# State space input products from stacked 96-row operands, and the skip term on VectorE

## The chip, the cores and the metric

One core of one Trainium2 chip. The metric is the device time of one execution in microseconds, the median of the runs; a profiled execution of the same program gives the trace. TensorE multiplies, VectorE and ScalarE work elementwise, GpSimd here issues a few DMAs and clears buffers, and SyncE issues most DMAs.

## What is computed

Two layers of a hybrid block on 272 rows (16 learned tokens and 256 of the input) of width 1024. A layer is: half a SwiGLU FFN (width 2816), a token mixer, another half FFN. The mixer runs one input projection, and two branches from it: forgetting attention with 8 heads, and a state space branch (S5). Cut to what the change touches, the state space branch is:

```python
# u: (L, 512), 32 groups of 16 channels, 64 complex states in each
bu_re = einsum('lgc,gpc->lgp', ug, b_re)      # the input products
bu_im = einsum('lgc,gpc->lgp', ug, b_im)
...                                           # scaled, then a scan over l
y = einsum('lgp,gcp->lgc', h_re, c_re) - einsum('lgp,gcp->lgc', h_im, c_im) \
    + d_skip.reshape(32, 16) * ug             # the skip term
y = gelu(y.reshape(L, 512))
z = y @ w_glu
out = z[..., :512] * sigmoid(z[..., 512:])
```

## The kernel before

Activations are held transposed: 128 channels on the partitions, the 272 rows along the free dimension. Every float32 product is made of three products of rounded parts (a high part and the rest, `hi` and `lo`): high by high, high by low, low by high. Lines 296 to 298 (`unit`) issue these for all large weights: one unit is 8 blocks of 128, so 24 matmuls. The weights stream from HBM through SyncE in file order; `Weights.high` (L156, ScalarE) rounds a unit and `Weights.low` (L169, VectorE) subtracts to get its low half, three to four units ahead of its use.

The order of instructions is written by the program itself. `tick()` is called after a unit: it prepares the weights of a later unit, runs the functions that `later(n, ...)` put off to this tick, and then lets the background go on. The background is a generator that yields a cost after each of its steps; a tick gives it a budget (900 in the FFN, 1600 in the Q, K, V stage, 2700 and 2600 beside the gates), and a yield of -1 ends its turn for this tick. `mids` are functions that run in the middle of the next unit of 8 blocks (at i == MID == 6), which is where the matmuls of the background stand. `finish_background()` runs whatever is left of it at once.

In the first FFN of layer 0 the background makes constants of the state space model (`ssm_setup`) and then the tables of layer 0 (`ssm_tables(0)`): the matrix B in two parts (`Bh`, `Bl`), powers for the rotations (`E`, by doubling, L599 to L609, with a squaring of 11 small operations between doublings), the output matrix (`Cx`, L617 to L631), and a diagonal matrix of the skip weights in two parts (`Dh`, `Dl`, L635 and L637). The FFN has 68 ticks (two for each of 22 column blocks, three for each of 8 output blocks), and the background starts at the eighth. The second FFN of layer 0 makes the tables of layer 1 in the same way, without the setup.

In the mixer the background is `ssm_branch`. A layer has 16 steps j in four blocks m. Step j: `bu` makes the input products, three matmuls for the real and three for the imaginary part, on the 32 partitions of `uh(m)`, `ul(m)` that belong to j; VectorE rotates them (`turn`, L676 into `p`), adds and subtracts (L728, L730), scans (L740) and rotates back (L676 into `m`). The next step's `bu` is asked for when the rotation into `p` is done, since there is one PSUM buffer for it. After four steps `out_m` makes an output block: three matmuls with the diagonal matrix for the skip term (L658 to L660) and 24 with `Cx` (L666), which ScalarE stores (L698). After the Q, K, V units (f, V0 to V3, eight of K and Q) and 16 gate units come two `branch_b` units, then `finish_background`, GELU and the GLU product.

`uh`, `ul` and `yr` (output) are slots of 128x4x272 from a pool of 18, given out in order of return.

Of the kernel before, what the change touches and what calls it, by code (L numbers as in the profile page):

```python
# [7 lines left out]
F32 = mybir.dt.float32  # L8
# [31 lines left out]
WARM = 10  # L40
START = 8
BLOCK = 1024
MASKED = -float(2.0 ** 100)
O_U, O_Q, O_K, O_V, O_F, O_G = 0, 512, 1024, 1536, 2048, 2056
MAGIC = 12582912.0
# [133 lines left out]
def body(tc, nc, ins, out):  # L179
    v, s, pe = nc.vector, nc.scalar, nc.tensor  # L180

    with (
# [7 lines left out]
    ):  # L190
        names = iter(range(10**6))

        halves = Slots(mp, "m", 18, [P, 4, T])
        banks = Slots(pp, "ps", 6, [P, 512])
        temps = Slots(tp, "t", 6, [P, T])
        bank, tmp = banks.take, temps.take
# [1 line left out]
        def big(n, dt=F32):  # L198
            return Tiles(halves, n, dt)
# [330 lines left out]
            yield SMALL  # L530

        E = cp.tile([P, 2, NJ, TS + 1], F32, name="E")
        Bh = cp.tile([P, 2, 4, P], F32R, name="Bh")
        Bl = cp.tile([P, 2, 4, P], F32R, name="Bl")
        Cx = cp.tile([P, 4, NJ, 32], F32, name="Cx")
        Dh = cp.tile([P, 4, P], F32R, name="Dh")
        Dl = cp.tile([P, 4, P], F32R, name="Dl")

        def ssm_tables(l):

            js = slice(l * NJ, (l + 1) * NJ)
            bslot = halves.take()
            Bm = bslot.rearrange("p a t -> p (a t)")[:, : 8 * P].rearrange("p (r m c) -> p r m c", r=2, m=4)
            nc.sync.dma_start(Bm, ins["B"][l])
            yield -1
            yield -1
            for r in range(2):
                s.copy(Bh[:, r], Bm[:, r])
                yield -1
                v.tensor_sub(Bl[:, r], Bm[:, r], Bh[:, r].bitcast(F32))  # L550
                yield 600
            halves.give(bslot)
            cslot = halves.take()
            Cm = cslot.rearrange("p a t -> p (a t)")[:, : 2 * NJ * 32].rearrange("p (r j c) -> p r j c", r=2, j=NJ)
            nc.sync.dma_start(Cm, ins["C"][l])
# [75 lines left out]
            v.tensor_scalar(Cx[:, 3], Cx[:, 2], -1.0, None, ALU.mult)  # L631
            yield 600
            halves.give(cslot)
            for m in range(4):
                s.activation(Dh[:, m], ident, AF.Copy, scale=pc("d", l, m))  # L635
                yield -1
                v.scalar_tensor_tensor(Dl[:, m], ident, pc("d", l, m), Dh[:, m].bitcast(F32), ALU.mult, ALU.subtract)  # L637
                yield 200


        def ssm_branch(l, uh, ul, yr, t0, ready):
            n = T - t0

            def bu(j):
                pb = bp.tile([P, 2, 512], F32, tag="b2", name=f"bu{next(names)}")
                m, q = divmod(j, 4)
                rows = slice(32 * q, 32 * q + 32)
                for r in range(2):
                    a, b, x, y = Bh[rows, r, m, :], Bl[rows, r, m, :], uh(m)[rows], ul(m)[rows]
                    pe.matmul(pb[:, r, :T], lhsT=a, rhs=x, start=True, stop=False)  # L650
                    pe.matmul(pb[:, r, :T], lhsT=a, rhs=y, start=False, stop=False)  # L651
                    pe.matmul(pb[:, r, :T], lhsT=b, rhs=x, start=False, stop=True)  # L652
                return pb

            def out_m(m, qt):
                ps = bank()
                a, b, x, y = Dh[:, m], Dl[:, m], uh(m)[:, t0:], ul(m)[:, t0:]
                pe.matmul(ps[:, :n], lhsT=a, rhs=x, start=True, stop=False)  # L658
                pe.matmul(ps[:, :n], lhsT=a, rhs=y, start=False, stop=False)
                pe.matmul(ps[:, :n], lhsT=b, rhs=x, start=False, stop=False)  # L660
                for x, row, a, b, stop in (
                    (0, 3, t0, TS, False), (3, 2, t0, TS, False), (1, 3, TS, T, False), (2, 2, TS, T, False),
                    (0, 0, t0, T, False), (2, 1, t0, T, True),
                ):
                    for q in range(4):
                        pe.matmul(  # L666
                            ps[32 * q : 32 * q + 32, a - t0 : b - t0], lhsT=Cx[:, x, 4 * m + q, :],
                            rhs=qt[q][:, row, a:b], start=False, stop=stop,
                        )
# [12 lines left out]
            pbs = {}  # L682

            def ask(j):
                mids.append(lambda: pbs.__setitem__(j, bu(j)))

            def shut(m, qt):


                def finish():  # L690
                    if not banks.free:
                        mids.append(finish)
                        return
                    ps = out_m(m, qt)
                    halves.give(*qt)

                    def store():
                        s.copy(yr(m)[:, t0:], ps[:, :n])  # L698
                        stored.append(m)
                        banks.give(ps)  # L700

                    later(1, store)

                mids.append(finish)

            while 0 not in ready:
                yield -1
            ask(0)
            g, qt = None, []
            for j in range(NJ + 1):  # L710
                back = iter(())
                if j < NJ:
                    p = buf("p", 1, [P, 4, T])
                    while j not in pbs:
                        yield -1
                    yield from turn(p, pbs.pop(j)[:, :, :T], j)
                    if j + 1 < NJ:
                        assert (j + 1) // 4 in ready
                        ask(j + 1)
                if j:  # L720
                    while not halves.free:
                        yield -1
                    qt.append(halves.take())
                    back = turn(qt[-1], g, j - 1)
                    yield next(back)
                if j < NJ:
                    c, d = (x.rearrange("p r (s t) -> p (r s) t", s=2) for x in (p[:, :2], p[:, 2:]))
                    v.tensor_add(c[:, 1:3], c[:, 1:3], d[:, 3::-3])  # L728
                    yield 352
                    v.tensor_sub(c[:, 0::3], c[:, 0::3], d[:, 2:0:-1])  # L730
# [18 lines left out]
        def mixer(l, hh, hl, t0, finish):  # L749
# [10 lines left out]
                    v.scalar_tensor_tensor(dst[:, lo:], ps[:, : T - lo], by, rstd[:, lo:], ALU.mult, ALU.mult)  # L760
                banks.give(ps)

            ready = set()

            def have_u(ps, m):
                u = tmp()
                scaled(ps, u, 0)

                def done():
                    temps.give(u)  # L770
                    ready.add(m)

                split(uh(m), ul(m), u, done)

            state["bg"] = ssm_branch(l, uh, ul, yr, t0, ready)
            state["budget"] = QKV_BUDGET
            for m in range(4):
                if m == 0:
# [267 lines left out]
                stored.clear()  # L1046

            bias(0)
            yb = big(8, F32R)
            gB, gA = big(8), None  # L1050
            for i in range(16):
                state["budget"] = GATE_BUDGET if i < 11 else LATE_BUDGET
# [15 lines left out]

                later(1, e)
                if 5 <= i < 12 and i % 2 == 1:  # L1070
                    values((i - 5) // 2)
                if 3 <= i < 11:
                    flip(i - 3)
# [38 lines left out]
            flush()  # L1112
            gelus()
            flush()
            for x in (uh, ul, yr):
                x.give()

            zg = big(8, F32R)
            for m in range(4):
# [287 lines left out]


def _ssm_mats(inp):
    B = np.zeros((DEPTH, P, 2, 4, P), np.float32)  # L1410
    C = np.zeros((DEPTH, P, 2, NJ, 32), np.float32)
    for r, (kb, kc) in enumerate((("ssm_b_re", "ssm_c_re"), ("ssm_b_im", "ssm_c_im"))):
        for gi in range(2):
            b = inp[kb].reshape(DEPTH, 4, 4, 2, 64, 16)[:, :, :, gi]
            for q in range(4):
                rows = slice(q * 32 + gi * 16, q * 32 + gi * 16 + 16)
                B[:, rows, r, :, gi * 64 : gi * 64 + 64] = b[:, :, q].transpose(0, 3, 1, 2)
            c = inp[kc].reshape(DEPTH, NJ, 2, 16, 64)[:, :, gi]
            C[:, gi * 64 : gi * 64 + 64, r, :, gi * 16 : gi * 16 + 16] = c.transpose(0, 3, 1, 2)
    return B, C  # L1420


# [26 lines left out]
```

## Time and profile before

| | |
|---|---|
| median of 3 runs | 1227.82 us (1227.7 to 1228.13) |
| profiled execution | 1226.46 us |
| its span, first to last instruction | 1224.7 us |
| mean granted clock of TensorE | 0.998 of full speed |
| TensorE busy | 1212.0 us, 99% |
| VectorE busy | 928.7 us, 76% |
| ScalarE busy | 637.1 us, 52% |

The difference between the profiled execution and its span, 1.76 us, lies around the first and last instruction. Busy times of TensorE are of pipelined matmuls whose ends are modelled: successive starts are 0.12 us apart where one takes 0.29 us in the rows, so starts are what to compare.

### The profile page before, as it was taken

Reading aid. Unit: us, or ns where it says so; the run is one execution under the profiler, and the core shown is the slowest. Engines: PE = TensorE matmul, PEld = TensorE weight load, DVE = VectorE, ACT = ScalarE, POOL = GpSimd, SP = SyncE. Lnnn points to the kernel's source line nnn. Section 1 sums busy time; section 2 is a strip of 40 time slices with the busy share of each in tenths; the row PEclk is TensorE's granted clock in tenths of the full one; section 3 lists DMA queues with packets and bytes.
Section 4 is the critical chain, followed back from the end, with each engine's and each line's share of the span. In section 5 each row is a group of like instructions: output and inputs, shape, how many; then the busy total and the mean of one; then the engine's idle time right before and its main releaser. Section 6 shows DMA issues by size and latency. Waiting matters only on the chain.

```text
span 1224.7 us, 24247 instructions
## 1 busy us (share of the span) xinstructions
PE 1212.0 (99%) x9905; PEld 1183.3 (97%) x9905; DVE 928.7 (76%) x1718; ACT 637.1 (52%) x1056; POOL 6.0 (0%) x12
## 2 busy tenths in 40 slices
PE   9999999999999999999999999999999999999997
PEld 8999999999889999999999999999998999999997
DVE  6978898998888798886565555559989897666553
ACT  7544444636557564444454444446475676544542
POOL 0000000000000000000000000000000000000000
PEclk9999999999999999999999999999999999999999
DMA  7756554543334665555556555554422355655551
GB/s 236 214 195 192 160 175 153 164 135 98 88 104 155 205 193 188 173 168 172 177 172 177 176 176 166 172 160 154 140 100 97 111 173 172 224 189 183 173 183 65
DMA packets 56479, 199.27 MB, mean 163 GB/s; under 512 B 6288, under 2 KB 6672, under 8 KB 56368
## 3 DMA queue, kind: packets, MB, share of 16 engines
q1 hardware_dynamic: 55872, 196.96, 51.5%
q8 instruction: 77, 1.26, 0.4%
q10 hardware_dynamic: 416, 0.62, 0.1%
q14 instruction: 34, 0.28, 0.1%
q0 software_dynamic: 80, 0.15, 0.0%
HBM read 196.66 MB, written 1.05 MB: 161 GB/s over the span
## 4 chain that ended last, share of the span: by engine, by line
PE 94%; DVE 3%; ACT 1%; issue 1%; DMA 1%; SPq 0%; DVEq 0%; ACTq 0%
PE ps L296 29%; PE ps L298 29%; PE ps L297 28%; PE ps L666 1%; DVE wl L169 1%; PE bu L650 1%; PE ps L965 1%; PE bu L651 1%; PE bu L652 1%; DMA raw<-wts 1%; PE ps L968 0%; ACT wh L156 0%; ACT m L1089 0%; PE ps L1030 0%; DVE p L676 0%
## 5 line engine op out<-in xcount | busy, mean ns | idle before, releaser
L296 PE MATMUL ps<-m,wh 128*128 128x272 f32 (+2 forms) x2960 | 856.5, 289 | 0.8 <-ACT wh L156 0.6
L298 PE MATMUL ps<-m,wl 128*128 128x272 f32 (+2 forms) x2960 | 849.5, 287 | 0.4 <-DVE wl L169 0.4
L297 PE MATMUL ps<-m,wh 128*128 128x272 f32 (+2 forms) x2960 | 847.0, 286 | 0.6 <-DVE m L315 0.3
L156 ACT CAST wh<-raw 128x1024 fp32r<-128x1024 f32 (+2 forms) x380 | 388.6, 1025 | 451.3 <-issue 235.6
L296 PEld LDWEIGHTS ps<-m,wh 128*128 128x128 f32 (+1 forms) x2960 | 556.3, 188 | 10.8 <-issue 5.6
L297 PEld LDWEIGHTS ps<-m,wh 128*128 128x128 f32 (+1 forms) x2960 | 556.2, 188 | 1.9 <-DVE m L315 0.8
L298 PEld LDWEIGHTS ps<-m,wl 128*128 128x128 f32 (+1 forms) x2960 | 556.4, 188 | 1.1 <-DVE wl L169 0.9
L169 DVE TENSOR_TENSOR wl<-raw,wh 128x1024 fp32r<-128x1024 f32 (+2 forms) x380 | 450.2, 1186 | 54.6 <-PE ps L298 43.9
L389 DVE TENSOR_TENSOR t<-t,ps 128x272 f32<-128x272 f32 (+1 forms) x88 | 38.1, 433 | 77.0 <-PE ps L298 75.2
L383 DVE TENSOR_TENSOR t<-ps,rstd 128x272 f32<-128x272 f32 (+1 forms) x88 | 38.3, 436 | 43.5 <-PE ps L298 42.9
L676 DVE TENSOR_TENSOR p<-bu,E 128x544 f32<-128x544 f32 x64 | 44.4, 719 | 8.6 <-PE bu L652 6.3
L676 DVE TENSOR_TENSOR m<-g,E 128x544 f32<-128x544 f32 x64 | 45.7, 717 | 2.7 <-PE ps L666 2.7
L740 DVE TENSOR_TENSOR_SCAN g<-ssm_mag,p 128x272 f32<-128x272 f32 x64 | 42.8, 710 | 0.7
L391 ACT CAST m<-t 128x272 fp32r<-128x272 f32 (+1 forms) x88 | 36.1, 410 | 12.6 <-DVE t L389 12.5
L417 DVE TENSOR_TENSOR t<-ps,rstd 128x272 f32<-128x272 f32 (+1 forms) x32 | 14.0, 437 | 36.9 <-PE ps L298 36.6
L394 DVE TENSOR_TENSOR m<-t,m 128x272 fp32r<-128x272 f32 (+1 forms) x88 | 37.9, 431 | 3.6 <-ACT m L391 3.6
L384 ACT ACTIVATE t<-t 128x272 f32<-128x272 f32 (+1 forms) x88 | 37.1, 422 | 6.1 <-DVE t L383 6.0
L329 ACT ACTIVATE m<-h,par 128x272 fp32r<-128x272 f32 (+1 forms) x48 | 24.5, 518 | 12.5 <-DVE h L419 7.2
L332 DVE SCALAR_TENSOR_TENSOR m<-h,par,m 128x272 fp32r<-128x272 f32 (+1 forms) x48 | 23.4, 494 | 8.5 <-ACT m L329 8.3
L354 DVE RECIPROCAL rstd<-t 128x272 f32<-128x272 f32 (+1 forms) x6 | 11.0, 1836 | 21.4 <-ACT t L353 21.4
L312 ACT CAST m<-t 128x272 fp32r<-128x272 f32 (+1 forms) x32 | 13.1, 415 | 19.9 <-DVE t L1167 15.4
L650 PE MATMUL bu<-m,Bh 32*128 32x272 f32 x64 | 21.4, 335 | 2.0 <-DVE p L676 2.0
(228 smaller groups left out, 709.1 us busy)
## 6 DMA issues: line engine op xcount, KB each, us to landing
raw<-wts SPq DMA_DIRECT2D x344, 512.0 KB, 3.6
raw<-wts SPq DMA_DIRECT2D x32, 384.0 KB, 3.4
h<-hT SPq DMA_DIRECT2D x4, 272.0 KB, 5.0
m<-B SPq DMA_DIRECT2D x2, 512.0 KB, 4.8
m<-C SPq DMA_DIRECT2D x2, 512.0 KB, 5.0
out<-m SPq DMA_DIRECT2D x2, 256.0 KB, 2.1
out<-m ACTq DMA_DIRECT2D x1, 512.0 KB, 2.8
raw<-wts SPq DMA_DIRECT2D x2, 128.0 KB, 2.0
```

The source lines that it names most:

```text
L156: nc.scalar.copy(hi[:, c : c + w // parts], r[:, c : c + w // parts])
L169: nc.vector.tensor_sub(lo[:, k], r[:, k], hi[:, k].bitcast(F32))
L296: pe.matmul(ps[:width, :n], lhsT=a, rhs=mh, start=first and i == ks[0], stop=False)
L297: pe.matmul(ps[:width, :n], lhsT=a, rhs=ml, start=False, stop=False)
L298: pe.matmul(ps[:width, :n], lhsT=b, rhs=mh, start=False, stop=last and i == ks[-1])
L383: v.tensor_mul(x[:, :n], pg[:, :n], rstd[:, t0:])
L384: s.activation(y[:, :n], x[:, :n], AF.Silu)
L389: v.tensor_mul(y[:, :n], y[:, :n], pu[:, :n])
L391: s.copy(ah(f)[:, t0:], y[:, :n])
L394: v.tensor_sub(al(f)[:, t0:], y[:, :n], ah(f)[:, t0:].bitcast(F32))
L676: v.tensor_tensor(d[:, :, :, a : a + TS], x[:, :, a : a + TS].unsqueeze(1).to_broadcast([P, 2, 2, TS]), tab.unsqueeze(2).to_broadcast([P, ...
L740: v.tensor_tensor_scan(g[:, r], mg, p[:, r], 0.0, ALU.mult, ALU.add)
```

## The change

B is laid out on the host in 32 rows, and three copies of these rows are stacked to 96. On the chip, `ssm_tables` loads it in four parts; rows 0 to 63 are rounded (two high copies), and rows 64 to 95 become the low part. The input of a step is stacked in the same way: high, low, high. One matmul over 96 rows then sums what three matmuls over 32 rows did, so a step has two matmuls in place of six. The stacked inputs are made by DMAs from SBUF to SBUF on GpSimd's queue, twelve for each block m, into a slot of their own; block 0 is declared ready two ticks after its DMAs are issued (`DELAY`). The diagonal matmuls go, and the skip term is added in the store, on VectorE, from `u` kept in `yr`. The pool has 19 slots, and `yb` is taken later.

```diff
+BROWS = 96
+DELAY = 2
-        halves = Slots(mp, "m", 18, [P, 4, T])
+        halves = Slots(mp, "m", 19, [P, 4, T])
-        Bh = cp.tile([P, 2, 4, P], F32R, name="Bh")
-        Bl = cp.tile([P, 2, 4, P], F32R, name="Bl")
+        Bs = cp.tile([BROWS, NJ, 2 * P], F32R, name="Bs")
-        Dh = cp.tile([P, 4, P], F32R, name="Dh")
-        Dl = cp.tile([P, 4, P], F32R, name="Dl")
         def ssm_tables(l):
-            bslot = halves.take()
-            Bm = bslot.rearrange("p a t -> p (a t)")[:, : 8 * P].rearrange("p (r m c) -> p r m c", r=2, m=4)
-            nc.sync.dma_start(Bm, ins["B"][l])
-            yield -1
-            yield -1
-            for r in range(2):
-                s.copy(Bh[:, r], Bm[:, r])
-                yield -1
-                v.tensor_sub(Bl[:, r], Bm[:, r], Bh[:, r].bitcast(F32))
-                yield 600
-            halves.give(bslot)
+            top = BROWS - 32
+            for j in range(0, NJ, 4):
+                x = Bs[:, j : j + 4].rearrange("p j c -> p (j c)")
+                slots = halves.take(), halves.take(F32R)
+                raw, hi = (y.rearrange("p a t -> p (a t)")[:BROWS, : 8 * P] for y in slots)
+                nc.sync.dma_start(raw, ins["B"][l][:, j * 2 * P : (j + 4) * 2 * P])
+                yield -1
+                yield -1
+                s.copy(x[:top], raw[:top])
+                s.copy(hi[top:], raw[top:])
+                yield -1
+                v.tensor_sub(x[top:], raw[top:], hi[top:].bitcast(F32))
+                yield 1200
+                halves.give(*slots)
...
-            for m in range(4):
-                s.activation(Dh[:, m], ident, AF.Copy, scale=pc("d", l, m))
-                yield -1
-                v.scalar_tensor_tensor(Dl[:, m], ident, pc("d", l, m), Dh[:, m].bitcast(F32), ALU.mult, ALU.subtract)
-                yield 200
...
             def bu(j):
                 for r in range(2):
-                    a, b, x, y = Bh[rows, r, m, :], Bl[rows, r, m, :], uh(m)[rows], ul(m)[rows]
-                    pe.matmul(pb[:, r, :T], lhsT=a, rhs=x, start=True, stop=False)
-                    pe.matmul(pb[:, r, :T], lhsT=a, rhs=y, start=False, stop=False)
-                    pe.matmul(pb[:, r, :T], lhsT=b, rhs=x, start=False, stop=True)
+                    pe.matmul(pb[:, r, :T], lhsT=Bs[:, j, r * P : r * P + P], rhs=us[m](q)[:BROWS], start=True, stop=True)
+                if q == 3:
+                    us[m].give()
...
             def out_m(m, qt):
-                a, b, x, y = Dh[:, m], Dl[:, m], uh(m)[:, t0:], ul(m)[:, t0:]
-                pe.matmul(ps[:, :n], lhsT=a, rhs=x, start=True, stop=False)
-                pe.matmul(ps[:, :n], lhsT=a, rhs=y, start=False, stop=False)
-                pe.matmul(ps[:, :n], lhsT=b, rhs=x, start=False, stop=False)
...
                     def store():
-                        s.copy(yr(m)[:, t0:], ps[:, :n])
+                        y = yr(m)[:, t0:]
+                        v.scalar_tensor_tensor(y, y, pc("d", l, m), ps[:, :n], ALU.mult, ALU.add)
...
             def have_u(ps, m):
-                u = tmp()
-                scaled(ps, u, 0)
+                scaled(ps, yr(m), 0)
                 def done():
-                    temps.give(u)
-                    ready.add(m)
+                    x = big(4, F32R)
+                    for q in range(4):
+                        for i, part in enumerate((uh, ul, uh)):
+                            nc.gpsimd.dma_start(
+                                x(q)[32 * i : 32 * i + 32].bitcast(F32), part(m)[32 * q : 32 * q + 32].bitcast(F32)
+                            )
+                    later(DELAY if m == 0 else 0, lambda: us.__setitem__(m, x))
+                    if m == 3:
+                        uh.give()
+                        ul.give()
-                split(uh(m), ul(m), u, done)
+                split(uh(m), ul(m), yr(m), done)
...
-            yb = big(8, F32R)
+            yb = None
...
                 if 5 <= i < 12 and i % 2 == 1:
+                    yb = yb or big(8, F32R)
```

## Rows read from the trace of the kernel before

**Rows 1.** Part 1 of the page: busy time, share of the span, instructions.

```profile
PE 1212.0 (99%) x9905; PEld 1183.3 (97%) x9905; DVE 928.7 (76%) x1718; ACT 637.1 (52%) x1056; POOL 6.0 (0%) x12
```

**Rows 2.** Stretches, first to last rotation in each layer's mixer: length, busy times, clock.

```profile
224.10:361.40 137.30, 136.46 (x1152) 124.46 (x1153) 122.46 (x212) 72.99 (x163) 0.00 (x0) 1.00 0.38 114
...
837.20:969.60 132.40, 131.20 (x1123) 120.01 (x1123) 121.33 (x206) 72.84 (x160) 0.00 (x0) 1.00 0.35 117
```

**Rows 3.** VectorE's waits in these two stretches: us in total, times, longest.

```profile
DVE mx L975 <- PE ps L968: 4.5, 3, 2.1
...
DVE m L760 <- PE ps L298: 0.3, 1, 0.3
...
DVE mx L975 <- PE ps L968: 3.9, 3, 2.0
...
DVE m L886 <- PE ps L298: 0.6, 1, 0.6
```

**Rows 4.** Timeline of TensorE, one step's input products: start, us, what.

```profile
222.85 0.28 PE L298 MATMUL ps<-m,wl 128*32 128x272 f32 x1
223.07 0.39 PE L650 MATMUL bu<-m,Bh 32*128 32x272 f32 x1
...
224.01 0.31 PE L296 MATMUL ps<-m,wh 128*32 128x272 f32 x1
```

**Rows 5.** Timeline of TensorE, an output block.

```profile
268.55 0.29 PE L658 MATMUL ps<-m,Dh 128*128 128x272 f32 x1
...
269.02 2.05 PE L666 MATMUL ps<-m,Cx 128*32 128x136 f32 x48
```

**Rows 6.** VectorE by line and shape, 163 to 212 us: count, busy, mean ns, idle.

```profile
L169 DVE TENSOR_TENSOR wl<-raw,wh 128x1024 fp32r<-128x1024 f32 x12 | 14.6, 1219 | 0.6 <-issue 0.6
...
L417 DVE TENSOR_TENSOR t<-ps,rstd 128x272 f32<-128x272 f32 x6 | 2.6, 439 | 0.9 <-PE ps L298 0.7
...
L603 DVE TENSOR_TENSOR E<-vn 128x256 f32<-128x256 f32 x4 | 1.7, 424 | 0.1
...
L617 DVE TENSOR_TENSOR Cx<-m,ssm_kr 128x512 f32<-128x512 f32 x1 | 0.7, 684 | 0.0
...
L599 DVE TENSOR_TENSOR vn<-E,s_a 128x144 f32<-128x144 f32 x1 | 0.3, 300 | 0.0
...
L579 DVE TENSOR_TENSOR s_r<-s_r,s_dt 128x16 f32<-128x16 f32 x1 | 0.2, 168 | 0.0
```

**Rows 7.** Timeline of VectorE at the end of layer 0's first FFN.

```profile
211.12 1.13 DVE L637 SCALAR_TENSOR_TENSOR Dl<-rcon,par,Dh 128x128 fp32r<-128x128 f32 x4
```

**Rows 8.** Timeline of TensorE: unit u3's first low product, first of unit f.

```profile
217.96 0.29 PE L298 MATMUL ps<-m,wl 128*128 128x272 f32 x1
...
220.73 0.29 PE L296 MATMUL ps<-m,wh 128*32 128x272 f32 x1
```

**Rows 9.** GpSimd's DMA issue on the timeline; DMA issues, KB, us to landing.

```profile
2.45 0.54 POOL L1220 DMA_DIRECT2D m<-conr  x1
...
m<-conr POOLq DMA_DIRECT2D x1, 136.0 KB, 5.0
```

**Rows 10.** Timeline of VectorE around the last rotation of layer 0.

```profile
360.05 1.36 DVE L676 TENSOR_TENSOR m<-g,E 128x544 f32<-128x544 f32 x2
361.33 0.79 DVE L1088 TENSOR_TENSOR m<-m,rstd 128x272 f32<-128x272 f32 x2
362.03 1.14 DVE L315 TENSOR_TENSOR m<-m,m 128x272 fp32r<-128x272 f32 x3
363.09 1.22 DVE L169 TENSOR_TENSOR wl<-raw,wh 128x1024 fp32r<-128x1024 f32 x1
364.22 0.79 DVE L1088 TENSOR_TENSOR m<-m,rstd 128x272 f32<-128x272 f32 x2
```

**Rows 11.** Timeline of TensorE, start of the last output block, both layers.

```profile
363.90 0.29 PE L658 MATMUL ps<-m,Dh 128*128 128x272 f32 x1
...
971.19 0.28 PE L658 MATMUL ps<-m,Dh 128*128 128x256 f32 x1
```

**Rows 12.** Stretches at the end of the kernel: busy times, clock behind them.

```profile
1219.50:1220.00 0.50, 0.00 (x0) 0.00 (x0) 0.50 (x1) 0.43 (x1) 0.00 (x0) 1.00 0.00 0
1220.00:1220.50 0.50, 0.00 (x0) 0.00 (x0) 0.13 (x1) 0.50 (x2) 0.00 (x0) 0.50 0.27 102
```

More of the change, by code (lines that the diff above doesn't have):

```diff
@@ L633, in ssm_tables, with ssm_branch @@
             halves.give(cslot)
-            for m in range(4):
-                s.activation(Dh[:, m], ident, AF.Copy, scale=pc("d", l, m))
-                yield -1
-                v.scalar_tensor_tensor(Dl[:, m], ident, pc("d", l, m), Dh[:, m].bitcast(F32), ALU.mult, ALU.subtract)
-                yield 200
-        def ssm_branch(l, uh, ul, yr, t0, ready):
+        def ssm_branch(l, us, yr, t0):
             n = T - t0
@@ L646, in bu @@
                 m, q = divmod(j, 4)
-                rows = slice(32 * q, 32 * q + 32)
                 for r in range(2):
-                    a, b, x, y = Bh[rows, r, m, :], Bl[rows, r, m, :], uh(m)[rows], ul(m)[rows]
-                    pe.matmul(pb[:, r, :T], lhsT=a, rhs=x, start=True, stop=False)
-                    pe.matmul(pb[:, r, :T], lhsT=a, rhs=y, start=False, stop=False)
-                    pe.matmul(pb[:, r, :T], lhsT=b, rhs=x, start=False, stop=True)
+                    pe.matmul(pb[:, r, :T], lhsT=Bs[:, j, r * P : r * P + P], rhs=us[m](q)[:BROWS], start=True, stop=True)
+                if q == 3:
+                    us[m].give()
                 return pb
@@ L656, in out_m @@
                 ps = bank()
-                a, b, x, y = Dh[:, m], Dl[:, m], uh(m)[:, t0:], ul(m)[:, t0:]
-                pe.matmul(ps[:, :n], lhsT=a, rhs=x, start=True, stop=False)
-                pe.matmul(ps[:, :n], lhsT=a, rhs=y, start=False, stop=False)
-                pe.matmul(ps[:, :n], lhsT=b, rhs=x, start=False, stop=False)
-                for x, row, a, b, stop in (
-                    (0, 3, t0, TS, False), (3, 2, t0, TS, False), (1, 3, TS, T, False), (2, 2, TS, T, False),
-                    (0, 0, t0, T, False), (2, 1, t0, T, True),
+                for x, row, a, b, start, stop in (
+                    (0, 0, t0, T, True, False), (0, 3, t0, TS, False, False), (3, 2, t0, TS, False, False),
+                    (1, 3, TS, T, False, False), (2, 2, TS, T, False, False), (2, 1, t0, T, False, True),
                 ):
@@ L667, in out_m @@
                             ps[32 * q : 32 * q + 32, a - t0 : b - t0], lhsT=Cx[:, x, 4 * m + q, :],
-                            rhs=qt[q][:, row, a:b], start=False, stop=stop,
+                            rhs=qt[q][:, row, a:b], start=start, stop=stop,
                         )
@@ L704, in shut @@
                 mids.append(finish)
-            while 0 not in ready:
+            while 0 not in us:
                 yield -1
@@ L717, in ssm_branch @@
                     if j + 1 < NJ:
-                        assert (j + 1) // 4 in ready
+                        assert (j + 1) // 4 in us
                         ask(j + 1)
@@ L761, in scaled @@
                 banks.give(ps)
-            ready = set()
+            us = {}
             def have_u(ps, m):
-                u = tmp()
-                scaled(ps, u, 0)
+                scaled(ps, yr(m), 0)
                 def done():
-                    temps.give(u)
-                    ready.add(m)
-                split(uh(m), ul(m), u, done)
-            state["bg"] = ssm_branch(l, uh, ul, yr, t0, ready)
+                    x = big(4, F32R)
[9 more added lines that the diff above has]
+                split(uh(m), ul(m), yr(m), done)
+            state["bg"] = ssm_branch(l, us, yr, t0)
             state["budget"] = QKV_BUDGET
@@ L1114, in mixer @@
             flush()
-            for x in (uh, ul, yr):
-                x.give()
+            yr.give()
             zg = big(8, F32R)
@@ L1409, in _ssm_mats @@
 def _ssm_mats(inp):
-    B = np.zeros((DEPTH, P, 2, 4, P), np.float32)
+    B = np.zeros((DEPTH, 32, 4, 4, 2, P), np.float32)
     C = np.zeros((DEPTH, P, 2, NJ, 32), np.float32)
@@ L1414, in _ssm_mats @@
             b = inp[kb].reshape(DEPTH, 4, 4, 2, 64, 16)[:, :, :, gi]
-            for q in range(4):
-                rows = slice(q * 32 + gi * 16, q * 32 + gi * 16 + 16)
-                B[:, rows, r, :, gi * 64 : gi * 64 + 64] = b[:, :, q].transpose(0, 3, 1, 2)
+            B[:, gi * 16 : gi * 16 + 16, :, :, r, gi * 64 : gi * 64 + 64] = b.transpose(0, 4, 1, 2, 3)
             c = inp[kc].reshape(DEPTH, NJ, 2, 16, 64)[:, :, gi]
             C[:, gi * 64 : gi * 64 + 64, r, :, gi * 16 : gi * 16 + 16] = c.transpose(0, 3, 1, 2)
-    return B, C
+    return np.concatenate([B.reshape(DEPTH, 32, -1)] * (BROWS // 32), axis=1), C
 def kernel(**inputs):
```

## The prediction

> **What bounds the kernel now.** The page comes first: the matrix engine is busy for 99% of the span [rows 1], so a matmul less should be time less wherever nothing else is equally full. The second question is whether that holds where the edited matmuls run. They all lie in the two token-mixer stages, so I cut out, with the view by stretches, the part of each mixer from the first state-space rotation to the last. In both, VectorE is busy for about nine tenths of a stretch in which the matrix engine is full too [rows 2]. The waits of VectorE in the same stretches come to 14.1 us in layer 0 (8 rows, first and last shown) and 10.0 us in layer 1 (5 rows) [rows 3]; most are waits for a matmul, which faster matmuls will shorten. What is left, 137.3 - 14.1 = 123.2 us and 132.4 - 10.0 = 122.4 us, is VectorE work in a fixed order, and the change takes none of it away. So the reader is to see two nearly equal bounds: matmuls that the change makes shorter, and a VectorE queue that it lengthens and shifts.
>
> **The change part by part.**
>
> *Input products.* Today a step j issues six 32-row matmuls. The last ordinary matmul before them starts at 222.85, the next ordinary one at 224.01 [rows 4]: 1.16 us, of which 0.12 is an ordinary interval, so 1.04 us for six. Six intervals of 0.12 to 0.13 are 0.74; the other 0.3 is lost at the two changes between 128-row and 32-row matmuls (0.22 before the first, 0.21 after the last). After: two 96-row matmuls, 0.25 us if they follow an ordinary one without that loss, 0.56 if not. I take 0.25, a saving of 0.79 per step, 16 steps in a layer: 12.6 us; the other end is 7.7. The Trainium skill (TensorEngine Tiling, Key Properties) says that a change of tiling mode drains the array, and it lists 128, 64 and 32 rows as the modes; the 0.3 us agrees, and by that list 96 rows would run as 128. No row of 96 is in this trace.
>
> *Skip term.* Three of the matmuls of each output block go: 268.55 to 269.02 [rows 5], 0.375 us by intervals, four blocks: 1.5 us in a layer. In return the store becomes a VectorE operation out of PSUM, 0.44 us by the nearest row (L417) [rows 6], three before the last rotation, 1.3 us, and one behind it. On TensorE alone a layer gets 14.1 us shorter, 28 us in all. That is the gain if nothing else bounds; the rest of this part is why I expect a tenth of it.
>
> *Tables in layer 0.* Loading B takes four rounds in place of one, and each round gives the turn back three times: rotation tables that began at tick 27 of the first FFN begin at tick 39, by the budget of 900 a tick. Today the background ends just too late: the four L637 run together at 211.12, when `finish_background` empties it [rows 7]. Twelve ticks later means 33 steps left over there: 8 products of 128x256, 11 of 128x16, 6 of 128x144 and 8 of 128x512. With 0.42, 0.17, 0.30 and 0.68 us [rows 6] that is 3.4 + 1.9 + 1.8 + 5.4 = 12.5 us, 11.8 with the overlap of starts that these lines have. Behind them in VectorE's queue waits the low half of weight unit u3. It is done at 224.1; TensorE wants it at 217.96 [rows 8]. A stall of 6.1 us, and V0 starts at 225.01 - 1.04 + 6.1 = 230.1. Bounds: 0 if the tables were through, 6.1 as counted. In layer 1 they are through at tick 59 of 68, so nothing is left. ScalarE's eight copies and VectorE's four subtractions for B fit in the FFN's idle time; if that cover were gone they would cost some 13 us once.
>
> *The copies to stacked buffers.* 48 DMAs in a layer, on the otherwise empty GpSimd queue. The only rows for such DMAs are two loads at the start: 0.54 us to issue and 5.0 us to land for the larger [rows 9]. Step 0 needs three of them: 1.6 + 5.0 = 6.6 us after the first low half (about 228.3 in layer 0, 832.8 in layer 1), so 235 and 839.4. The first input product sits in unit V1, at about 235.2 and 842.2. Hidden, by nothing in layer 0 and by 3 us in layer 1; if step 0 waited for all twelve, 5 us later in each. Block 1 is needed more than 15 us later. I take 0 and keep +10 for the range. The Trainium skill (SBUF — State Buffer, Who interferes with whom) says that descriptor writing for GpSimd's DMAs is locked out while VectorE runs two-port copies or tensor_scalar; VectorE's work here is almost all two-input products, so I give that no price.
>
> *Delay.* The first step is asked for two ticks later (V1, not the f unit), so the same rotations end two ticks later, in the first `branch_b` tick. That puts in front of the last rotation a pair of L1088, three L315 and a weight subtraction that today come behind it: 361.33 to 364.22, 2.9 us [rows 10]. What waits for that rotation is the last output block, then GELU, then the GLU product.
>
> *The sum.* VectorE starts rotating at 235.7 in layer 0 and 842.7 in layer 1 (first product plus its end). From there: today's work, less 3.0 us now done before it (L315, L799 and two L169 of 1.22, overlapping), plus 2.9 displaced, plus 1.3 for stores, plus waits that remain. I take 2.5 and 2 us for those (bounds 0 and today's 14.1 and 10.0; small, because TensorE will be ahead).
> Layer 0: 235.7 + 123.2 - 3.0 + 2.9 + 1.3 + 2.5 = 362.6; the last block starts at 363.90 today [rows 11]: 1.3 us gained.
> Layer 1: 842.7 + 122.4 - 3.0 + 2.9 + 1.3 + 2.0 = 968.3; today 971.19 [rows 11]: 2.9 us gained.
> TensorE alone would be there at about 354 and 955: it idles for 8 and 13 us, spread over the input products (each waits for the rotation before it) and the last block. Behind the last block nothing changes: its way through store, GELU table, cast and subtraction is 6 us before and after.
>
> *Clock.* Idle TensorE has a price. Its last matmuls of the kernel lie before 1219; the granted clock is still 1.00 up to 1220.0 and 0.50, the lower of its two levels, after it [rows 12]. Three stalls of several microseconds (u3 and the two last blocks) can each cost up to half the matmuls that follow at the half level; between 0 and 1.5 us each by 2 to 3 us of such work, 4.5 in all. Much of it falls where VectorE is late anyway, so I take 1.3. The Trainium skill (TensorE: Matmul & The Clock Gate, Part 1) has the same two levels.
>
> Sum: -1.3 - 2.9 + 1.3 = -2.9 us on a profiled execution of 1226.46 (span 1224.7 and 1.76 around it), which is 1.36 below the median shown. On the median: 1227.8 - 2.9 = 1224.9.
>
> **The rivals.**
>
> *A. Nothing to see.* Clock losses of the full 4.5 us cancel the 4.2 us, or the switch loss stays with 96 rows and takes some. Speaks for it: both bounds are so close. Time 1227 to 1229. Chance 0.28.
>
> *B. Slower: step 0 waits for its transfers.* One mechanism: the gather for block 0 lands later than V1. VectorE has no idle time left to absorb it, so each microsecond beyond the sixth is one of the whole kernel, in each layer. From about 2 us lateness in both layers the gain is gone. With all twelve waited for, 5 us a layer: -2.9 + 10 = +7, 1235. For it: the landing of 5.0 us, and layer 0's zero margin. Against: loads of h in four parts are consumed part by part, so waits go by region. Chance 0.30, with it the case that the leftover tables cost more than counted.
>
> *C. TensorE was the only bound.* All 28 us, 1200. Needs the tables done in time and VectorE's waits to vanish beyond their 14 and 10 us. Speaks against it: 123 us of work in a stretch of 137. Half of it, 1214, would do if VectorE recovered. Chance 0.05.
>
> *D. The edit of B does not bind.* Leftover tables find cover (u3 not late): layer 0 gains 6 more, 1219. Speaks against it: the four L637 already stand behind the FFN. In C's 0.05 by weight, as part of faster.
>
> **How the numbers follow.** Forecast 0.37, own range 1221 to 1225.3; A 0.28; B 0.30; C and D 0.05. A measurement of this kernel tells about 0.2%, 2.5 us, from no change. Faster by more: 0.37 + 0.05 = 0.42; within: 0.28; slower by more: 0.30. The range goes from 1219 (D) to 1235 (B in full); outside it are C and a worse B.
>
> **What would show it.** Right: some 33 small VectorE operations between the FFN's last accumulation and the subtraction for u3, a TensorE gap of about 6 us near 218; each input product as two matmuls with 0.12 us starts and no 0.2 us gap around; VectorE without idle time from about 236 to 362; a wait of TensorE for the last rotation in both layers. Wrong: the first input product waiting for a DMA (B), no gap near 218 (D), a last block well before 360 and 965 (C), or VectorE idle for more than 6 us between first and last rotation, which would turn layer 0 into a loss.

## The result and the profile after

The changed kernel takes 1240.28 us in the median (1239.72 to 1240.98) against 1227.76 for the kernel before on the same chip: a ratio of 1.0107 (95% interval 1.0095 to 1.0119). The forecast was 1224.9, 1219 to 1235. The profiled execution has a span of 1238.2 us, 13.5 longer than before, at a mean granted clock of 0.986 (0.998 before).

Part 1 of the page, beside [rows 1]:

```profile
PE 1196.4 (97%) x9753; PEld 1170.0 (94%) x9753; DVE 937.1 (76%) x1722; ACT 645.1 (52%) x1052; POOL 53.1 (4%) x108
```

TensorE is busy for 15.6 us less and the span is longer, so TensorE waits. Where? A pair of norm matmuls (L351; L349 in the kernel before) stands once near the start of every FFN and mixer, so the first start of each pair divides the kernel. From there in a mixer to the same place in the FFN behind it lie 212.70 and 204.52 us before, 222.77 and 207.93 after; everything else agrees within 0.1. So 10.1 us were lost in layer 0's mixer and 3.4 in layer 1's. The view by stretches, before and then after (length, busy TensorE, weight loads, VectorE, ScalarE, GpSimd; clock; DMA share; GB/s):

```profile
214.23:426.93 212.70, 211.86 (x1779) 198.32 (x1778) 185.61 (x327) 124.17 (x248) 0.00 (x0) 1.00 0.45 134
827.29:1031.81 204.52, 202.81 (x1743) 189.50 (x1742) 183.10 (x321) 122.70 (x244) 0.00 (x0) 1.00 0.42 138
```

```profile
214.27:437.04 222.77, 202.93 (x1703) 190.95 (x1701) 196.85 (x358) 122.24 (x244) 23.59 (x48) 0.96 0.46 136
837.40:1045.33 207.93, 195.83 (x1667) 183.39 (x1666) 184.66 (x325) 120.74 (x240) 23.56 (x48) 0.97 0.44 143
```

TensorE idled for 0.8 and 1.7 us in the mixers before, and for 19.8 and 12.1 after. Some of its busy time is also matmuls at the lower of the clock's two levels, a granted clock of 0.50. Taken over all stretches of 2 us with a clock under 0.99, busy time times the missing share of the clock is 4.4 us in layer 0 and 5.4 in layer 1, against none before. That is an estimate, since busy time has modelled ends. Four of these stretches:

```profile
224.00:226.00 2.00, 1.96 (x8) 1.96 (x9) 2.00 (x3) 0.00 (x0) 0.00 (x0) 0.50 0.44 74
...
374.00:376.00 2.00, 2.00 (x17) 0.96 (x11) 0.08 (x1) 0.00 (x0) 0.00 (x0) 0.50 0.03 8
...
883.00:885.00 2.00, 2.00 (x12) 2.00 (x11) 2.00 (x4) 1.05 (x1) 0.00 (x0) 0.50 0.41 164
...
985.00:987.00 2.00, 2.00 (x35) 1.68 (x39) 2.00 (x5) 1.71 (x3) 0.00 (x0) 0.50 0.00 0
```

An account by layers follows; it closes by construction, since length is busy plus idle time, and only the share put down to the clock is estimated. Layer 0: 13.3 us less TensorE work (211.86 against 202.93 - 4.4), 19.0 more idle time, 4.4 of clock: +10.1. Layer 1: 12.4 less, 10.4 idle, 5.4 of clock: +3.4. The matmuls did become cheaper, nearly as forecast (14.1 a layer), and more than that was given back.

The waits of TensorE over the whole execution (us, times, longest):

```profile
PE ps L657 <- DVE m L667: 13.3, 4, 4.5
PE bu L645 <- issue: 9.2, 7, 2.6
PE ps L300 <- DVE wl L171: 6.3, 3, 5.9
```

All three end with VectorE. The first is the last output block waiting for its rotations. The second is an input product; the trace names no releaser, but the one PSUM buffer `bu` is free only when VectorE has rotated the step before. In the two longest of these waits that rotation ends at 259.26 and 881.88, and the product starts 0.1 us later. The third is weight unit u3 behind the leftover tables.

VectorE in layer 0, timeline at the end of the tables (beside [rows 7, 8]):

```profile
211.16 0.42 DVE L609 TENSOR_TENSOR vn<-E,s_a 128x256 f32<-128x256 f32 x1
...
222.43 0.43 DVE L633 TENSOR_SCALAR Cx<-Cx 128x512 f32<-128x512 f32 x1
222.77 1.22 DVE L171 TENSOR_TENSOR wl<-raw,wh 128x1024 fp32r<-128x1024 f32 x1
```

And TensorE, in the same layer, where it waits for that, at the first input product, and at the last output block (beside [rows 4, 11]):

```profile
224.04 0.59 PE L300 MATMUL ps<-m,wl 128*128 128x272 f32 x1 [5.88 <-DVE wl L171]
...
239.80 0.29 PE L300 MATMUL ps<-m,wl 128*128 128x272 f32 x1
239.93 0.42 PE L645 MATMUL bu<-m,Bs 96*128 96x272 f32 x2
240.18 0.29 PE L298 MATMUL ps<-m,wh 128*128 128x272 f32 x1
...
363.20 0.65 PE L657 MATMUL ps<-m,Cx 128*32 128x272 f32 x4
366.74 0.82 PE L657 MATMUL ps<-m,Cx 128*32 128x272 f32 x2 [2.89 <-DVE m L667]
372.05 3.83 PE L657 MATMUL ps<-m,Cx 128*32 128x272 f32 x42 [4.48 <-DVE m L667]
```

Two 96-row matmuls stand 0.25 us between their neighbours with no gap: the switch loss of [rows 4] is gone. At the end of the layer TensorE reaches the output block at 363.20, then stands 12.7 us over it, 10.6 more than the 2.05 of [rows 5]: 7.4 of them are the two waits shown, and the rest is mostly the half clock (42 matmuls in 3.83 us, 48 in 2.05 before).

Why is the rotation late? From first to last rotation, layer 0 and 1, beside [rows 2], and VectorE's waits there, beside [rows 3]:

```profile
241.12:371.99 130.87, 116.97 (x1027) 107.28 (x1025) 124.96 (x221) 70.24 (x156) 13.73 (x28) 0.98 0.41 119
852.98:984.92 131.94, 119.90 (x1022) 109.17 (x1020) 122.11 (x210) 68.73 (x154) 15.54 (x32) 0.96 0.37 122
```

```profile
DVE m L690 <- PE ps L657: 3.6, 2, 2.3
...
DVE m L690 <- PE ps L657: 7.3, 3, 3.7
DVE p L667 <- PE bu L645: 1.8, 2, 1.2
```

VectorE, which had become the longer queue, is itself idle for 5.9 and 9.8 us of these stretches. Most of it stands before the new store (L690), which waits for an output block. (Of the 1.8 us in the last row, 1.2 lie just ahead of the first rotation. The rest of the idle time is in gaps under 0.15 us, which the view of waits leaves out, and 0.2 us before another line.) One such place in layer 1, VectorE and then TensorE:

```profile
956.27 1.34 DVE L732 TENSOR_TENSOR_SCAN g<-ssm_mag,p 128x272 f32<-128x272 f32 x2
961.35 0.48 DVE L690 SCALAR_TENSOR_TENSOR m<-m,par,ps 128x256 f32<-128x256 f32 x1 [3.73 <-PE ps L657]
961.74 1.22 DVE L171 TENSOR_TENSOR wl<-raw,wh 128x1024 fp32r<-128x1024 f32 x1
```

```profile
959.33 1.94 PE L657 MATMUL ps<-m,Cx 128*32 128x256 f32 x48
```

VectorE is free at 957.6, the block ends at 961.3, and a weight subtraction and rotations that need nothing from it queue behind the store.

### The profile page after: what moved, and what is told of

Its sections match the earlier page's. It is cut to its first block, busy times and chain, and to the rows that moved or that the text cites. A ratio compares the mean times of both kernels' runs of the same rounds, so it can differ in the third digit from the quotient of the medians.

```text
span 1238.2 us, 24127 instructions
## 1 busy us (share of the span) xinstructions
PE 1196.4 (97%) x9753; PEld 1170.0 (94%) x9753; DVE 937.1 (76%) x1722; ACT 645.1 (52%) x1052; POOL 53.1 (4%) x108
## 4 chain that ended last, share of the span: by engine, by line
PE 88%; DVE 9%; issue 2%; DMA 1%; ACT 0%; SPq 0%; DVEq 0%; ACTq 0%
PE ps L298 28%; PE ps L300 28%; PE ps L299 28%; DVE wl L171 2%; PE ps L657 2%; DVE m L667 1%; DVE g L732 1%; DVE p L667 1%; PE bu L645 1%; DMA raw<-wts 1%; PE ps L965 0%; DVE p L722 0%; DVE p L720 0%; PE ps L1030 0%; DVE mx L975 0%
## 5 line engine op out<-in xcount | busy, mean ns | idle before, releaser
L765 POOL DMA_DIRECT2D m<-m x96 | 47.2, 497 | 47.3 <-ACT m L314 32.9
L393 ACT CAST m<-t 128x272 fp32r<-128x272 f32 (+1 forms) x88 | 36.2, 411 | 11.4 <-DVE t L391 11.3
L745 POOL MEMSET m<- 128x1088 f32 x4 | 4.0, 1008 | 770.3 <-PE ps L300 770.3
L657 PE MATMUL ps<-m,Cx 128*32 128x136 f32 (+3 forms) x384 | 22.5, 355 | 13.3 <-DVE m L667 13.3
L657 PEld LDWEIGHTS ps<-m,Cx 128*32 128x32 f32 x384 | 13.0, 120 | 19.2 <-DVE m L667 15.8
```

The lines of the kernel that those rows point to most:

```text
L657: pe.matmul(ps[32 * q : 32 * q + 32, a - t0 : b - t0], lhsT=Cx[:, x, 4 * m + q, :], rhs=qt[q][:, row, a:b], start=start, stop=stop,)
L765: nc.gpsimd.dma_start(x(q)[32 * i : 32 * i + 32].bitcast(F32), part(m)[32 * q : 32 * q + 32].bitcast(F32))
```

## The experiments

Three suspects came out of the profile, all in program order: the late tables (T), the place of the store (S), the delay of the first product (D). In the expectations, theory L is that the late tables are on the path, theory S the same of the store, and V the rival that VectorE's amount of work alone sets the end. The leftover steps also burden the planner's account: the 33 steps charge some 10,000 ns, which at 1600 a tick keeps the background silent for six ticks, and that is why the first product of layer 0 stands in unit V2, not V1. In the results "mixers" are the lengths from norm matmul to norm matmul, layer 0 and 1, in the profiled execution. Ratios are to the kernel before, with 95% intervals.

### Tables

**Tables in time.**

```diff
-    state = {"tick": 0, "bg": None, "credit": 0.0, "budget": FFN_BUDGET}
+    state = {"tick": 0, "bg": None, "credit": 0.0, "budget": 1200.0}
```

> The changed kernel with 1200 in place of 900 ns of background per tick in the first FFN, so that layer 0's rotation tables are through before its mixer begins; nothing else is changed. Theory L (late tables): of the 13.5 us that the changed kernel's profiled execution is longer, 10.1 lie in layer 0's mixer and 3.4 in layer 1's; without the burst layer 0 should lose what layer 1 loses, so about 6.7 us less: 1233.6. Rival V (VectorE's work from first to last rotation is the only cause, and the burst falls where VectorE is late anyway): 1238 to 1240.5.

1231.33 us, ratio 1.0033 (1.0021 to 1.0045); mixers 213.31 and 207.59. All of the gain of 9 us is in layer 0, which now loses 0.6 against before; layer 1 is within 0.4 us of where it was. Theory L holds, and its price is larger than the 5.9 us stall and than the 6.7 expected. The first rotation of layer 0 now stands as far behind the norm matmul as layer 1's (15.6 us), and VectorE's waits before stores there are 7.1 us in place of 3.6: behind late tables only half of the store's waits show.

**Late tables in the kernel before.**

```diff
-            yield -1
-            yield -1
+            for _ in range(2 + (10 if l == 0 else 0)):
+                yield -1
```

> The kernel before with ten more turns given back while layer 0's B is loaded, so that its tables end as late as in the changed kernel (account of the leftover steps about 8,400 ns against 9,700), with the old six-matmul products and no delay of the first step. Theory L: a TensorE stall of about 5 us for weight unit u3 and half the matmuls behind it at the half clock, 1.3 us, all of it on the path: about 1234. Rival: VectorE has 14.1 us of waits in the stretch behind it and makes the lateness good: 1228 to 1230.

1235.51 us, ratio 1.0069 (1.0054 to 1.0084); mixers 220.24 and 206.05. Lateness alone costs the old kernel 7.5 us in layer 0, with this wait of TensorE:

```profile
PE ps L298 <- DVE wl L169: 4.8, 1, 4.8
```

The clock is at 0.50 from 222 to 228 us, which by the estimate used above costs 2.8 us; with the wait of 4.8 that is the whole of the 7.5. The 14 us of VectorE waits behind it make nothing good. (Layer 1, whose code is the same, is 1.5 us longer in this execution; its clock fell, see the last section.)

**No debt.**

```diff
             finish_background()
+            state["credit"] = 0.0
```

> The changed kernel with the planner's account set to zero when the leftover tables are through, so that their cost (about 10,000 ns on the account) no longer keeps the first rotation of layer 0 out of one more tick; the burst itself stays. Theory L: the first input product moves from unit V2 to V1 and the rotations end one tick earlier, 3.1 us: about 1237. Rival V: the same VectorE work stands in front of the last output block, only in another order, 1239.5 to 1240.5. The TensorE stall of 5.9 us for weight unit u3 must be there in both.

1239.54 us, ratio 1.0103 (1.0087 to 1.0118); mixers 222.75 and 207.82. The first rotation starts at 238.40 in place of 241.12, and the last ends at 371.84 in place of 371.99. Counted from the norm matmul, which is 0.35 us earlier in this trace, the start is 2.4 us earlier and the end 0.2 later. Taking the account away gains nothing; that part of Theory L falls. VectorE's waits before stores in that stretch are 7.4 us in place of 3.6, which takes up the earlier start. TensorE's matmuls at the lower clock cost more in this mixer too (about 7 us in place of 4.4, by the same estimate), so the run doesn't show that the account is harmless in every order.

### The store

**Store behind the rotations of its tick.**

```diff
-                    later(1, store)
+                    later(1, lambda: tail(store))
```

> The changed kernel with the store of an output block (VectorE, out of PSUM) put behind the rotations of its tick in place of ahead of them. Theory S: VectorE stands 3.6 us in layer 0 and 7.3 us in layer 1 before the store, waiting for the output block, with rotations queued behind it; if that is on the path, 5 to 10 us come back: 1230 to 1235. Theory L and V: these waits only take the place of waits that VectorE would have for TensorE anyway: 1239 to 1241.

1233.0 us, ratio 1.0052 (1.0035 to 1.0069); mixers 221.28 and 202.55. Layer 1 gains 5.4 us and is 2.0 faster than before; VectorE's wait before stores there falls from 7.3 to 0.6 us:

```profile
DVE m L690 <- PE ps L657: 0.6, 1, 0.6
```

Theory S holds. In layer 0 only 1.5 us come back, behind the late tables. (The edit moves the store behind a weight subtraction as well as the rotations, as both stood behind it in the tick.)

**Both edits.**

```diff
-    state = {"tick": 0, "bg": None, "credit": 0.0, "budget": FFN_BUDGET}
+    state = {"tick": 0, "bg": None, "credit": 0.0, "budget": 1200.0}
...
-                    later(1, store)
+                    later(1, lambda: tail(store))
```

> The changed kernel with both edits: tables in time and the store behind the rotations of its tick. If the two causes are separate, their gains add (9.0 and 7.3 us of 1240.3): 1224. If both only uncover the same VectorE bound, the smaller of them is lost: 1229 to 1232.

1219.75 us, ratio 0.9942 (0.9927 to 0.9957); mixers 210.65 and 201.60, in a profiled execution of 1222.01 us, the slowest of its four. Both mixers are now shorter than before. The two gains alone would give 1224, and the run is 4.3 us better: neither edit uncovers only what the other had, but the two are not independent either, as each is worth more beside the other.

**Only the skip term, in the kernel before.**

```diff
-                pe.matmul(ps[:, :n], lhsT=a, rhs=x, start=True, stop=False)
-                pe.matmul(ps[:, :n], lhsT=a, rhs=y, start=False, stop=False)
-                pe.matmul(ps[:, :n], lhsT=b, rhs=x, start=False, stop=False)
...
-                        s.copy(yr(m)[:, t0:], ps[:, :n])
+                        y = yr(m)[:, t0:]
+                        v.scalar_tensor_tensor(y, y, pc("d", l, m), ps[:, :n], ALU.mult, ALU.add)
```

> The kernel before with only the skip term moved: the three 128-row matmuls of an output block go, and the store becomes a VectorE operation ahead of the rotations of its tick, as in the change; the six-matmul products stay (the tables of the old skip matmuls are still made, as before). TensorE alone: 1.5 us a layer less, 1225. Theory S: VectorE, which stands next to its own limit, waits in its queue for each output block, 3 to 7 us a layer, of which the 14.1 and 10.0 us of waits that it has today hide a part: 1229 to 1235.

1226.12 us, ratio 0.9993 (0.9983 to 1.0002): no change, and Theory S's number is wrong here. VectorE does wait as it says, in layer 0:

```profile
DVE m L695 <- PE ps L662: 8.7, 3, 4.5
```

But TensorE waits only 1.2 us for VectorE in that stretch (0.8 before). Not all of TensorE's saving arrives: an output block is 0.37 us shorter, 2.9 us in all eight, and by the medians the run is 0.8 us faster. So the same place of the store costs some 2 us (1 to 3 by the interval) while TensorE is the slower queue, and 7.3 once it is the faster one.

### The delay and the gathers

**No delay, and nothing else.**

```diff
-DELAY = 2
+DELAY = 0
```

> The changed kernel with the delay of the first input product taken away and nothing else. In layer 0 the account of the leftover tables keeps the first rotation where it was, so only layer 1 can gain: about 3 us by the pair of runs with and without the delay (201.6 to 198.3 us for layer 1's mixer), 1237. If the gathers were late without the table and store edits (rival B): 1241 or more.

1235.08 us, ratio 1.0067 (1.0052 to 1.0082); mixers 222.85 and 202.19. Layer 1 gains 5.7 us, more than expected; layer 0 nothing, as the account says. In layer 1 TensorE no longer waits at the last output block (5.9 us with the delay); its waits at input products grow from 3.3 to 7.4, 1.9 of them for a gather.

**Both edits (tables and store), and a delay of one tick.**

```diff
-DELAY = 2
+DELAY = 1
```

> As the first run of this set, with the first input product delayed by one tick (unit V0). The gathers land about 1 us before it. If the start of VectorE's rotations counts: 3 us a layer, 1218. If the order of VectorE's work decides (as the run without the debt shows for one tick in layer 0, 0.7 us): 1223 to 1224.

1214.76 us, ratio 0.9897 (0.9881 to 0.9914); mixers 204.78 and 199.96. That is 5.0 us less than with two ticks, and no product waits for a transfer: the start of the rotations counts.

**Both edits, and no delay.** As before, with DELAY = 0.

> As the run before, with the first input product not delayed (unit f in place of V1). Rival B (the gathers): the first three transfers issue until about 844.7 in layer 1 and land 4 us later, the product stands at about 846.1, so TensorE waits some 2.5 us in each layer: 1224 plus 5, less what the earlier start of VectorE gives (2 to 6 us): 1223 to 1229. If the gathers are early enough and VectorE's start is what counts: 1218 or less.

1212.77 us, ratio 0.9882 (0.9867 to 0.9897); mixers 205.33 and 198.29. The gathers are late by 1.5 and 0.8 us, and that is all; TensorE at the first input product of each layer, with GpSimd's issues for layer 0:

```profile
224.67 0.49 PE L645 MATMUL bu<-m,Bs 96*128 96x272 f32 x2 [1.48 <-DMA m<-m]
...
829.64 0.49 PE L645 MATMUL bu<-m,Bs 96*128 96x272 f32 x2 [0.76 <-DMA m<-m]
```

```profile
218.67 0.51 POOL L765 DMA_DIRECT2D m<-m  x1 [12.99 <-ACT m L314]
220.05 3.91 POOL L765 DMA_DIRECT2D m<-m  x8 [0.87 <-DVE m L317]
```

The third issue ends at about 221.0 and the product goes at 224.67. Starting VectorE two ticks earlier brings 7.0 us with these waits of 2.2 already paid. TensorE now waits for no rotation at the last output block; its time in the two mixers is 199.51 of 205.33 and 191.83 of 198.29 us.

**Tables and no delay, the store left ahead.** The budget of 1200 in the first FFN, DELAY = 0, and the store as the change has it.

> The changed kernel with tables in time and without the delay, the store where the change has it (ahead of the rotations). If the store's place costs what it did with the delay (1231.3 against 1219.75): 1224 to 1225. If an earlier start of VectorE already takes away its waits for output blocks: 1213 to 1217.

1220.71 us, ratio 0.9945 (0.993 to 0.9959); mixers 208.25 and 203.24. That lies between the two expected ranges. The store's place costs 7.9 us here, against 11.6 with the delay (1231.33 against 1219.75). VectorE's waits before stores are 6.4 and 6.3 us, against 7.1 and 7.3: an earlier start takes away a part of the price and little of the waits.

### The order within the mixer

**Both edits, the delay of two ticks, larger budgets.**

```diff
-QKV_BUDGET = 1600.0
-GATE_BUDGET = 2700.0
-LATE_BUDGET = 2600.0
+QKV_BUDGET = 1900.0
+GATE_BUDGET = 3000.0
+LATE_BUDGET = 2900.0
```

> As the first run of this set, with 300 ns more of background per tick in the mixer (1900, 3000, 2900), so that the last rotation is ordered two ticks earlier, ahead of the first branch_b unit's VectorE work (2.9 us by rows of before). If that displacement is on the path: 3 us or more a layer, 1217 to 1219. If TensorE then waits for the low halves of its weights instead: 1223 to 1227.

1218.63 us, ratio 0.9929 (0.9914 to 0.9944); mixers 207.92 and 201.67. About 1 us better than with the tables and the store alone; the time lies in the range of the first case only because the run that it builds on was 4 us faster than was then expected. TensorE no longer waits at the last output block (2.9 and 4.1 us without this edit), but 2.6 and 2.2 us more at the input products. The displaced 2.9 us of the prediction are a small matter beside the start of the rotations.

**All three edits, a smaller budget in the Q, K, V stage.**

```diff
-QKV_BUDGET = 1600.0
-GATE_BUDGET = 2700.0
+QKV_BUDGET = 1450.0
+GATE_BUDGET = 2800.0
```

> All three edits (tables in time, store last, no delay), and 150 ns less of background per tick up to the first gates, 100 ns more after them: the sixth input product, for which TensorE waits 3.3 and 3.6 us for VectorE in the run without this, comes one tick later. If that wait and the half clock behind it are on the path: 1208 to 1211. If the rotations then end later by as much: 1212 to 1215.

1212.49 us, ratio 0.9888 (0.9871 to 0.9904); mixers 204.13 and 198.56, no different in the median from the run with all three edits. In the profiled execution (1211.5 us; the four lie between 1211.41 and 1214.8) the clock is 1.00 throughout both mixers, where the other run lost 1.7 and 3.0 us by the same estimate. Layer 0 is 1.2 us shorter; in layer 1 TensorE idles for 8.7 us in place of 6.5, and the gain is gone. So the half clock was not all that kept it from being faster. That the later input product causes this idle time is likely, but not shown.

## Why the prediction was wrong

**Input products and skip matmuls: right.** 0.25 us for two 96-row matmuls was taken and 0.25 stands in the trace; an output block is 0.37 us shorter (0.375 taken); the 12.4 to 13.3 us less TensorE work in a mixer answer to the 14.1 forecast. By the Trainium skill's list of tiling modes (TensorEngine Tiling, Available Configurations) 96 rows would run in the mode of 128; the missing gap agrees.

**VectorE as the second bound: right.** The named sign, a wait for the last rotation in both layers, is there, and all three waits of TensorE end with VectorE. What its order costs is shown by the edits: the same matmuls with VectorE's queue in another order give 1212.77 in place of 1240.28.

**"Waits that remain", 2.5 and 2 us: the step that failed, above all in layer 1.** By the same view as the 14.1 and 10.0 they are 3.6 and 8.1 us inside the stretches (idle time with the shortest gaps is 5.9 and 9.8). In layer 1 that explains why the stretch is 131.9 us and not 125.6. In layer 0 it explains 1.1 us of 4.0 (0.7 more is the reading below, the rest is not separated), but the store's waits there are 7.1 once the tables are in time. The text said that the waits would be small "because TensorE will be ahead". It priced the store as 0.44 us of work (0.49 measured) and forgot that it is also a wait, put ahead of rotations in an in-order queue. The prediction listed no such rival. Moving it gives 5.4 us in layer 1. The last sign of being wrong, VectorE idle for more than 6 us, is met in layer 1; layer 0, which lost more, stays just under it. A small error of reading stands beside this: 0.7 us of the 14.1 and of the 10.0 lie ahead of the first rotation, so VectorE's work was taken 0.7 too small.

**Tables: the burst right, its price too small, the step that failed in layer 0.** All 33 steps stand behind the FFN, VectorE finished u3's half at 224.0 (forecast 224.1) and TensorE waited 5.9 us (6.1). But 13 matmuls behind it ran at 0.23 us in place of 0.13, 1.3 us, and the planner's account, not looked at, moved the first product from V1 to V2. First rotation: 241.12 in place of 235.7. Without the account nothing was gained, but with the tables in time the whole of the lateness gives 9 us back, where 6.1 had been counted (rival D). How these 9 divide beyond the stall was not separated in the changed kernel; in the kernel before, the stall and the half clock were all of it.

**Start in layer 1, gathers: right.** The first rotation is at 852.98, less the 10.1 lost before it 842.9 (forecast 842.7). No wait for a transfer stood at the first product, and none in the run with a delay of one tick. In the runs without the delay the gathers cost 0.8 to 1.9 us a layer, and those runs are faster all the same. Slower it was, but not by B's mechanism; the half sentence in B on leftover tables that cost more than counted is the part that came true, and its 0.30 had no price for them.

**Delay: too cheap.** It was priced by 2.9 us of work displaced. Its real price is that VectorE starts two ticks later and TensorE waits at the other end: 5.7 us in layer 1 alone, by the run without it, and 7.0 us in all beside the other two edits.

**Clock: mis-sized.** 1.3 us (at most 4.5) was taken, from three stalls. No matmul of the kernel before runs at the lower level, so no row stood behind the 2 to 3 us of such work for each stall; behind u3 it was 3.1 us. By the estimate above, 9.8 us were lost in all. Waits at input products can let the clock fall as well: it fell after 2.64 us before the one at 881.99, and stayed after 2.09 before the one at 259.36.

The sum, layer 0: start +5.4, stretch 130.9 in place of 126.9, +4.0, the last block at the half clock +1.8; 11.2 on a forecast of -1.3 makes 9.9, against 10.1 measured. Layer 1: start +0.2, stretch 131.9 for 125.6, +6.3, block +1.6 (42 matmuls in 3.54 us); 8.1 on a forecast of -2.9 makes 5.2, against 3.4. Of the 1.8 us between, 1.4 lie behind the last output block, where the prediction had no change: the same 480 matmuls up to the next norm matmul take 56.9 us in place of 58.3.

Rival C, all 28 us, was reached by no run. With tables in time, the store behind the rotations and an early start 14.8 us of it are there, about the 1214 that C gave for half of it. These three edits bring 27.5 us together and 9.0, 7.3 and 5.2 one by one. Three smaller parts of the change (the 19th slot, `yb` taken later, the gathers' own issue) were not taken out singly; all are in the run at 1212.77, so they don't cause the loss.

## What to carry to other kernels

When an edit makes the fuller of two nearly full engines cheaper, redo the order for the other engine: every wait that stood hidden in its queue now has a price. An operation that reads another engine's result is a wait as well as work, so put it behind whatever does not need it. Work that is put off "to be safe" (a delay, a table spread over more turns) should be priced by what starts late because of it.

## What the runs showed of the hardware

- Among 128-row matmuls, where nothing is waited for, a 96-row matmul starts 0.12 to 0.13 us after its neighbour, as one of 128 rows does. Six 32-row matmuls in the same place take 1.16 us from neighbour to neighbour, 0.28 more than seven such intervals.
- GpSimd's SBUF to SBUF gathers (34 KB) took 0.50 us each to issue and landed in 4.0 us (median; 1.7 to 6.2), beside a VectorE that was busy for 95% (layer 0) and 93% (layer 1) of the time between first and last rotation.
- A wait of TensorE of 1.2 us for the rotation buffer stands in layer 1 of the kernel before, and again in the same code with late tables. In the first the clock stayed at 1.00; in the second it fell to 0.50 in the third stretch shown:

```profile
880.00:882.00 2.00, 0.93 (x8) 0.72 (x7) 1.97 (x4) 0.00 (x0) 0.00 (x0) 1.00 0.13 41
882.00:884.00 2.00, 1.88 (x13) 1.76 (x14) 2.00 (x4) 0.06 (x1) 0.00 (x0) 0.96 0.58 221
884.00:886.00 2.00, 2.00 (x11) 2.00 (x10) 2.00 (x6) 0.99 (x1) 0.00 (x0) 0.50 0.44 127
886.00:888.00 2.00, 2.00 (x14) 2.00 (x14) 2.00 (x3) 0.00 (x0) 0.00 (x0) 0.69 0.45 166
```

So the same wait was followed by no loss in one execution and by 1.7 us of lost matmul time (the estimate above) in another; a single profile doesn't settle what a short wait costs.
